# Pairs in the first gate/up block, un-normed operands, and weight sums moved to GpSimd in a transformer block

## The chip, the core and the metric

The kernel runs on one core of one Trainium2 chip. The metric is the device time of one execution in microseconds. The core has five engines that matter here, each with its own queue of instructions that it works off in order: TensorE (PE, matmuls and transposes), VectorE (DVE), ScalarE (ACT), GpSimd (POOL) and the sync engine (SP), which only issues transfers. Engines wait for each other by semaphores.

## The reference

One layer of a hybrid transformer on 256 rows of width 2048, in float32:

```python
h = x + W_out [ DiffAttn(heads) ; ConformerConv(channels) ] ( RMSNorm(x) )
hn = rms_norm(h, norm2_g)                   # h * rsqrt(mean(h*h) + eps) * gain
a  = hn @ w_gate                            # 2048 x 5632
bu = hn @ w_up                              # 2048 x 5632
y  = h + (silu(a) * bu) @ w_down            # 5632 x 2048
```

The change concerns the last four lines, from the point at which h is complete. The norm's factor is one number for each row of h (called rstd2 in the kernel); the gain is one number for each column. So (h * gain) @ w, multiplied by rstd2 row by row afterwards, is the same as hn @ w.

## The kernel before, in words

**Products.** Every float32 product is made of three: each operand is split into a high part in a reduced format (fp32r) and the rest, and x @ w is x_hi w_hi + x_lo w_hi + x_hi w_lo. The rows of h are the stationary operand (two halves of 128 rows, m = 0 and 1), transposed, in 16 slices k of 128 columns. The weights are the moving operand, 512 columns at a time.

**Chunks.** The weights come in chunks of two slices k of 512 columns (128x1024 elements). A chunk is fetched by SP into `raw`, rounded by ScalarE into `whi` (L326), its rest is made by VectorE as `wlo` (L335), and TensorE has 12 products of it (two slices, two halves, three products). For some chunks ScalarE and a GpSimd transfer make `wlo` in VectorE's place (`by_dma`: ScalarE writes the negative of the rounded weights, L329, then a transfer adds `raw`, L330).

**Pairs.** From block 1 on, four of the sixteen slices of gate and up go through a fast scheme: a `pair` takes slice k and slice k+8, gate and up, and needs seven block products (each of three) where plain chunks need eight, so 21 TensorE instructions in place of 24. For it the weights need four sums (`wt`: L1049 with 1024 elements, L1050 and L1051 with 512, of the four raw parts `wb`), the rounding of three raw parts and four sums (`wh`: L1052, L1055) and their rests (`wlb` L1058, `wlt` L1059). The operands of h need seven forms (`make_forms`). The products gather in eight PSUM banks `q`, and after a block's last pair VectorE makes the results from them (`bank_sums`, L1188 to L1193).

**Blocks.** The feed-forward part has eleven gate/up blocks j = 0 to 10 of 512 columns of gate and up each, in groups of 4, 4 and 3; behind each group stand two passes over w_down. A fast block consists of four pairs (s) and eight plain chunks of gate (g) and up (u); their order is a string, `sggsggsuusuu`, and for block 1 `gsggsgsuusuu`. Block 0 is plain before: sixteen chunks with the operands `hhi`, `hlo`, since the forms aren't there yet.

**How block 0 opens.** `out_done(n)` runs when 512 columns of h are complete in PSUM (n = 0 to 3): VectorE adds x (L828), TensorE transposes (L846), ScalarE copies with the gain into `hn` (L851) and casts to `hhi` (L853), VectorE makes `hlo` (L854). For n = 3 also the squares (L479), rstd2, and a copy of h to DRAM (`hd`, by GpSimd). The factor is applied in block 0 after the products (`silu_done`, `up_done`). Meanwhile `make_forms` turns rstd2 into a row through TensorE (`ps_r`), multiplies `hn` by it (L996) and makes `chi`, `clo` and the seven forms for the blocks that follow.

**What sets the order.** The program is written out by a scheduler of generators. It steps through the chunks; for each it first makes the loads, the rounding (`round`) of chunks up to three ahead and the rests (`split`) of chunks up to two ahead, then the products, with a `resume()` in between, which moves every running generator (`out_done`, `make_forms`, `bank_sums` and the like) one `yield` further. `yield from lag(n)` waits n such steps. Each engine then executes its own instructions in exactly that order.

Of the kernel before, what the change touches and what calls it, by code (L numbers as in the profile page):

```python
# [18 lines left out]
P = 128  # L19
# [14 lines left out]
LINE = 128  # L34
EPS = 1e-6
# [51 lines left out]
FIRST_ORDER = "gsggsgsuusuu"  # L87
# [42 lines left out]
def tile_block(  # L130
# [13 lines left out]
    prestack = ExitStack()  # L144
    pre = prestack.enter_context(tc.tile_pool(name="pre", bufs=2))
    small = prestack.enter_context(tc.tile_pool(name="small", bufs=4))
# [4 lines left out]
    h = [pre.tile([P, D], F32, tag=f"h{m}", name=f"h{m}", bufs=1) for m in range(NM)]  # L151
# [325 lines left out]
    def square_sum(src, accum, **kw):  # L477
        junk = pre.tile([P, N], F32, tag="junk", name="junk", bufs=1)
        act.activation(junk[:, : src.shape[-1]], src, AF.Square, accum_out=accum, **kw)  # L479
# [106 lines left out]
    def conv_back(b):  # L586
# [37 lines left out]
        for b in range(2):  # L624
            for t in range(NB // 2):
# [6 lines left out]
                for j in range(2):  # L632
# [3 lines left out]
                    hi = pre.tile([P, S], F32R, tag="mchi", name=f"mchi{ct}", bufs=NCT)  # L636
                    lo = pre.tile([P, S], F32R, tag="mclo", name=f"mclo{ct}", bufs=NCT)
# [135 lines left out]
    def attend_values(hd):  # L773
# [29 lines left out]
        for e in range(2):  # L803
            mixa[2 * hd + e] = lhs_pair("a", 2 * hd + e) if hd >= 2 else tuple(
                pre.tile([P, S], F32R, tag=t, name=t, bufs=4) for t in ("mahi", "malo"))
# [7 lines left out]
    hT = {}  # L813

    hn = []
# [9 lines left out]
    def out_done(n, ps):  # L825
        cs = slice(n * N, (n + 1) * N)
# [13 lines left out]
        for t in range(0, N // P, 2):  # L840
# [6 lines left out]
            if k % HK == 0:  # L847
                hn.append(early.tile([P, HK, S], F32, tag="wb", name="hn"))
            rows = hn[k // HK][:, k % HK : k % HK + 2, :]
            for i in range(2):  # L850
                act.activation(rows[:, i, :], pt[:, i, :], AF.Copy, scale=col("g2", k + i))  # L851
            hi, lo = lhs_two("h", k)
            act.copy(hi, rows)  # L853
            dve.tensor_tensor(lo, rows, hi.bitcast(F32), ALU.subtract)  # L854
            for i in range(2):
                hT[k + i] = (hi[:, i, :], lo[:, i, :])
# [3 lines left out]
        else:  # L860
            yield
            yield
            prestack.close()
            ffn["pool"] = ctx.enter_context(tc.tile_pool(name="ffn", bufs=1))
            start(make_forms())


    ffn = {}
    actT = {}
    sil = {}  # L870

    def silu_done(ps):
        yield
        for m in range(NM):
            sil[m] = ffn["pool"].tile([P, N], F32, tag=f"sum{m}", name="sil")
            act.activation(sil[m], ps[m], AF.Silu, scale=rstd2[m])

    def up_done(j, ps):
# [190 lines left out]
    def multiply_pair(c):  # L1069
        while (fs := c["pairs"]()) is None:  # L1070
            resume()
# [304 lines left out]
```

## The time and the profile before

| | |
|---|---|
| Median of 3 runs | 1032.63 us (1032.61 to 1032.65) |
| Profiled execution, span from first to last instruction | 1030.8 us |
| Profiled execution, time around the span | not shown for itself; the median less the span is 1.8 us |
| TensorE busy | 1025.7 us (100%) |
| VectorE busy | 929.2 us (90%) |
| ScalarE busy | 643.4 us (62%) |
| GpSimd busy | 102.7 us (10%) |
| Granted TensorE clock | 1.000 |

A row of a timeline gives the start in us, the time of the instruction (or of a run of like ones, x4), engine, line, operation, what it writes and reads, the shape, and in brackets how long the engine had been idle and what ended that. TensorE's instructions overlap: a 512-column product is shown with 0.39 us and the next starts 0.23 us later. VectorE's and ScalarE's overlap a little with their follower on the same engine. A row of a window gives the stretch, the sum and the busy time of each engine (with counts), the granted clock, the share of the transfer engines and their rate.

### The profile page before, as it was taken

The numbers are of one execution on the slowest core, as the hardware profiler recorded it, in microseconds if no ns is written. First come the engines' busy times: TensorE is split into PE (matmuls) and PEld (weight loads), VectorE is DVE, ScalarE is ACT, GpSimd is POOL, SyncE is SP. The second block draws the span as 40 slices with busy tenths as digits, with TensorE's granted clock in tenths as the row PEclk, the third lists the DMA queues.
The fourth block names the chain that finished last, engine by engine and source line by source line (L and its number), as shares of the span: only waits on it lengthen the run. The fifth ranks groups of instructions, "written<-read, shape, count | busy, mean of one in ns | idle before, by whom it ended". The sixth has DMA issues, their size and how long they took to land.

```text
span 1030.8 us, 13034 instructions
## 1 busy us (share of the span) xinstructions
PE 1025.7 (100%) x4642; PEld 849.4 (82%) x4642; DVE 929.2 (90%) x1128; ACT 643.4 (62%) x786; POOL 102.7 (10%) x146
## 2 busy tenths in 40 slices
PE   9999999999999999999999999999999999999998
PEld 8888888888888888888888888888888888888887
DVE  6899999999765699999999898989999989889998
ACT  7644656665756675676666556667757556657562
POOL 0300112111000000100102101101001111010020
PEclk9999999999999999999999999999999999999999
DMA  9757555544466677997989799889798979897776
GB/s 338 254 194 258 190 184 164 158 169 166 141 215 214 197 262 222 282 265 210 254 259 272 251 257 270 258 234 262 228 269 255 285 207 283 247 267 218 226 200 174
DMA packets 116448, 238.64 MB, mean 232 GB/s; under 512 B 7840, under 2 KB 9120, under 8 KB 116384
## 3 DMA queue, kind: packets, MB, share of 16 engines
q1 hardware_dynamic: 105216, 203.58, 59.3%
q0 software_dynamic: 10880, 34.08, 17.0%
q8 instruction: 36, 0.59, 0.2%
q14 instruction: 28, 0.23, 0.1%
q10 hardware_dynamic: 288, 0.16, 0.1%
HBM read 204.24 MB, written 9.44 MB: 207 GB/s over the span
## 4 chain that ended last, share of the span: by engine, by line
PE 100%; POOL 0%; DVE 0%; issue 0%; POOLq 0%
PE acc L365 11%; PE acc L366 11%; PE acc L371 11%; PE q L1097 11%; PE q L1103 11%; PE q L1098 11%; PE q L1078 9%; PE q L1077 9%; PE q L1076 9%; PE ps_a L898 1%; PE ps_s L712 1%; PE ps_o L782 1%; PE ps_warm L164 0%; PE ps_h L846 0%; PE ps_qk L693 0%; PE ps_at L802 0%
## 5 line engine op out<-in xcount | busy, mean ns | idle before, releaser
L326 ACT CAST whi<-raw 128x1024 fp32r<-128x1024 f32 (+1 forms) x256 | 264.2, 1043 | 143.8 <-PE acc L366 86.6
L335 DVE TENSOR_TENSOR wlo<-raw,whi 128x1024 fp32r<-128x1024 f32 (+1 forms) x208 | 250.4, 1214 | 38.2 <-ACT whi L326 38.0
L1055 ACT CAST wh<-wt 128x2048 fp32r<-128x2048 f32 x61 | 116.8, 1915 | 109.9 <-DVE wt L1051 109.7
L1059 DVE TENSOR_TENSOR wlt<-wt,wh 128x2048 fp32r<-128x2048 f32 x61 | 139.8, 2291 | 19.8 <-ACT wh L1055 19.7
L1097 PE MATMUL q<-whi,chi 128*128 128x512 f32 x320 | 125.2, 391 | 0.0
L1098 PE MATMUL q<-whi,clo 128*128 128x512 f32 x320 | 124.6, 389 | 0.0
L365 PE MATMUL acc<-whi,xhi 128*128 128x512 f32 x312 | 124.1, 398 | 0.0
L366 PE MATMUL acc<-whi,xlo 128*128 128x512 f32 x312 | 122.2, 392 | 0.0
L1076 PE MATMUL q<-wh,fhi 128*128 128x512 f32 x280 | 109.8, 392 | 0.0
L1077 PE MATMUL q<-wh,flo 128*128 128x512 f32 x280 | 109.0, 389 | 0.0
L1058 DVE TENSOR_TENSOR wlb<-wb,wh 128x1536 fp32r<-128x1536 f32 x61 | 106.8, 1751 | 1.0 <-ACT wh L1052 1.0
L572 DVE SCALAR_TENSOR_TENSOR y<-upad,cw,y 128x256 f32<-128x256 f32 x240 | 101.6, 490 | 0.0
L330 POOL DMA_DIRECT2D wlo<-raw x48 | 41.5, 865 | 555.7 <-ACT wlo L329 286.3
L1052 ACT CAST wh<-wb 128x1536 fp32r<-128x1536 f32 x61 | 89.8, 1472 | 1.0 <-DMA wb<-in_w_down_dram 1.0
L1103 PE MATMUL q<-wlo,chi 128*128 128x512 f32 x320 | 85.7, 390 | 0.0
L371 PE MATMUL acc<-wlo,xhi 128*128 128x512 f32 x312 | 85.2, 394 | 0.0
L1049 DVE TENSOR_TENSOR wt<-wb 128x1024 f32<-128x1024 f32 x61 | 74.4, 1220 | 0.0
L1097 PE MATMUL q<-whi,ahi 128*128 128x512 f32 x182 | 71.0, 390 | 0.0
L1098 PE MATMUL q<-whi,alo 128*128 128x512 f32 x182 | 70.9, 389 | 0.0
L1103 PEld LDWEIGHTS q<-wlo,chi 128*128 128x128 f32 x320 | 60.0, 188 | 12.7 <-DMA wlo<-raw 0.3
L1097 PEld LDWEIGHTS q<-whi,chi 128*128 128x128 f32 x320 | 60.1, 188 | 12.3
L1098 PEld LDWEIGHTS q<-whi,clo 128*128 128x128 f32 x320 | 60.1, 188 | 12.2
(260 smaller groups left out, 1850.5 us busy)
## 6 DMA issues: line engine op xcount, KB each, us to landing
raw<-in_w_in_dram SPq DMA_DIRECT2D x78, 512.0 KB, 4.6
raw<-in_w_gate_dram SPq DMA_DIRECT2D x48, 512.0 KB, 5.0
raw<-in_w_up_dram SPq DMA_DIRECT2D x48, 512.0 KB, 5.3
wlo<-raw POOLq DMA_DIRECT2D x48, 512.0 KB, 7.1
raw<-in_w_down_dram SPq DMA_DIRECT2D x46, 512.0 KB, 6.2
wb<-in_w_down_dram SPq DMA_DIRECT2D x42, 512.0 KB, 5.9
wb<-in_w_up_dram SPq DMA_DIRECT2D x40, 512.0 KB, 4.4
wb<-in_w_gate_dram SPq DMA_DIRECT2D x40, 512.0 KB, 5.5
```

Of the source, the lines that this page charges most:

```text
L326: act.copy(c["hi"], c["raw"])
L335: dve.tensor_tensor(c["lo"], c["raw"], c["hi"].bitcast(F32), ALU.subtract)
L365: pe.matmul(ps[m], xhi[:, ms], hi[:, j, :], start=c["first"] and j == 0, stop=False)
L366: pe.matmul(ps[m], xlo[:, ms], hi[:, j, :], start=False, stop=False)
L371: pe.matmul(ps[m], xhi[:, ms], lo[:, j, :], start=False, stop=c["last"] and j == nk - 1)
L1055: act.copy(c["hi"][:, :SUMMED], c["t"])
L1059: dve.tensor_tensor(lot, c["t"], c["hi"][:, :SUMMED].bitcast(F32), ALU.subtract)
L1076: pe.matmul(ps, hi, c["hi"][:, w], start=bool(first), stop=False)
L1077: pe.matmul(ps, lo, c["hi"][:, w], start=False, stop=False)
L1097: pe.matmul(ps, xs[i][0][:, ms], hi[:, i, :], start=i == 0 and bool(c["first"].get(qs[m])), stop=False)
L1098: pe.matmul(ps, xs[i][1][:, ms], hi[:, i, :], start=False, stop=False)
L1103: pe.matmul(sum_bank(c, qs[m]), xs[i][0][:, ms], lo[:, i, :], start=False, stop=i == 1 and bool(c["last"].get(qs[m])))
```

## The change

What it does, in the order of the program:

1. **Operands without the factor.** The transposed h with the gain, but not rstd2, is written by ScalarE straight to `chi`, the rest by VectorE to `clo` (for the slices of the plain chunks), and to `rows` for the slices of the pairs. `make_forms` starts when three quarters of h are complete, since the pairs' slices lie in the first three quarters, and has no factor, no `ps_r` and no multiplication any more. rstd2 is applied in `products_done` of every block: Silu with the factor as its scale, then a copy of the result with the same scale (the products of gate and up each carry the factor once).
2. **Pairs in block 0.** Block 0 is a fast block with the order `gugsgsgsusuu`; its PSUM banks come from the two pools the other way round (`swap`), and no wlo is made by a transfer in it. `round_pair` steps the generators until the forms and the memory (`late`) are there.
3. **A pair's VectorE work** is cut into smaller pieces and interleaved: 1024 elements of `wt` in `round_pair`, then `wlb` 512, `wt` 512, `wlb` 1024, `wt` 512, and `wlt` in two halves of 1024. ScalarE casts the sums in two halves too.
4. **Bank sums** in an order in which no sum needs the one just ahead of it, but for the first ones.
5. **GpSimd** makes the three `wt` sums of the next pair that hasn't been rounded (`sums_aside`), written out behind the bank sums; that holds for 14 of the 65 pairs.
6. The memory pools are laid out anew: what was freed at once before block 0 is freed in two steps, at the first and the last 512 columns of h.

```diff
-FIRST_ORDER = "gsggsgsuusuu"
+ORDERS = {0: "gugsgsgsusuu", 1: "gsggsgsuusuu"}
...
     def out_done(n, ps):
+        if not n:
+            prestack.close()
+            ffn["pool"] = fp = ctx.enter_context(tc.tile_pool(name="ffn", bufs=1))
...
-            if k % HK == 0:
-                hn.append(early.tile([P, HK, S], F32, tag="wb", name="hn"))
-            rows = hn[k // HK][:, k % HK : k % HK + 2, :]
-            for i in range(2):
-                act.activation(rows[:, i, :], pt[:, i, :], AF.Copy, scale=col("g2", k + i))
-            hi, lo = lhs_two("h", k)
-            act.copy(hi, rows)
-            dve.tensor_tensor(lo, rows, hi.bitcast(F32), ALU.subtract)
+            if k % HK < NS:
+                rows = ffn["rows"][:, k // HK, k % HK : k % HK + 2, :]
+                for i in range(2):
+                    act.activation(rows[:, i, :], pt[:, i, :], AF.Copy, scale=col("g2", k + i))
+            else:
+                a = REST.index(k)
+                hi, lo = (ffn[x][:, a : a + 2, :] for x in ("chi", "clo"))
+                for i in range(2):
+                    act.activation(hi[:, i, :], pt[:, i, :], AF.Copy, scale=col("g2", k + i))
+                for i in range(2):
+                    dve.scalar_tensor_tensor(lo[:, i, :], pt[:, i, :], col("g2", k + i), hi[:, i, :].bitcast(F32),
+                                             ALU.mult, ALU.subtract)
+                    plain[k + i] = (hi[:, i, :], lo[:, i, :])
             yield
...
+        if n == HK * P // N:
+            yield
             start(make_forms())
+        if n == D // N - 1:
+            yield
+            yield
+            keepstack.close()
+            ffn["late"] = ctx.enter_context(tc.tile_pool(name="late", bufs=1, side="right"))
...
     def round_pair(c):
-        assert "pair" in forms
+        while "pair" not in forms or "late" not in ffn:
+            resume()
...
+    def first_sums(c, engine):
+        b = c["b"]
+        c["t"] = t = ffn["pool"].tile([P, 4, N], F32, tag="wt", name="wt")
+        engine.tensor_tensor(t[:, 2:4], b[:, 1:3], b[:, 0:1].to_broadcast([P, 2, N]), ALU.subtract)
+
+    def last_sums(c, engine):
+        b, t = c["b"], c["t"]
+        yield engine.tensor_tensor(t[:, 1], b[:, 1], t[:, 3], ALU.add)
+        yield engine.tensor_tensor(t[:, 0], t[:, 1], b[:, 3], ALU.subtract)
+
+    def sums_aside():
+        pairs = [c for c in chunks if c.get("kind") == "s"]
+        n = next((n for n, c in enumerate(pairs) if not c.get("rounded")), None)
+        if n and "b" in pairs[n] and "lo" in pairs[n - 1]:
+            c = pairs[n]
+            first_sums(c, pool)
+            c["summed"] = len(list(last_sums(c, pool)))
...
     def split_pair(c):
-        act.copy(c["hi"][:, :SUMMED], c["t"])
...
-        dve.tensor_tensor(lob, c["b"][:, 1:], c["hi"][:, SUMMED:].bitcast(F32), ALU.subtract)
-        dve.tensor_tensor(lot, c["t"], c["hi"][:, :SUMMED].bitcast(F32), ALU.subtract)
+        act.copy(hi[:, 2:SUMMED], t[:, 2:])
+        rest(lob[:, :1], b[:, 1:2], hi[:, SUMMED : SUMMED + 1])
+        next(sums, None)
+        rest(lob[:, 1:], b[:, 2:], hi[:, SUMMED + 1 :])
+        next(sums, None)
+        act.copy(hi[:, :2], t[:, :2])
+        rest(lot[:, 2:], t[:, 2:], hi[:, 2:SUMMED])
+        rest(lot[:, :2], t[:, :2], hi[:, :2])
...
     def bank_sums(q):
         act.copy(w1, q[Q1])
         yield
         dve.tensor_tensor(u2, q[Q6], w1, ALU.add)
+        dve.tensor_tensor(w1, q[Q2], w1, ALU.add)
         dve.tensor_tensor(u3, q[Q7], u2, ALU.add)
+        dve.tensor_tensor(u2, q[Q5], u2, ALU.add)
         dve.tensor_tensor(w4, q[Q5], u3, ALU.add)
-        dve.tensor_tensor(u2, q[Q5], u2, ALU.add)
-        dve.tensor_tensor(w1, q[Q2], w1, ALU.add)
         dve.tensor_tensor(u3, q[Q4], u3, ALU.add)
+        sums_aside()
...
-        for t in g:
-            act.activation(t, t, AF.Silu)
+        for m, t in enumerate(g):
+            act.activation(t, t, AF.Silu, scale=rstd2[m])
+            act.activation(t, t, AF.Copy, scale=rstd2[m])
...
-            if j:
-                gate_up_block(j)
-                continue
-            block(w_gate, j * N, range(KD), fh, silu_done)
-            block(w_up, j * N, range(KD), fh, lambda ps, j=j: up_done(j, ps))
+            gate_up_block(j)
```

How it moves instructions, at three places: where block 0 begins, where it ends, and GpSimd's queue. Names end in the number of the buffer.

TensorE where block 0 begins, before: the last transposes of h (`ps_h`) stand in two groups of four; this is the first group, between the first and the second chunk of block 0 (`hhi`, `hlo`).

```order
L365 MATMUL acc<-whi,hhi_2958 128x512
L366 MATMUL acc<-whi,hlo_2959 128x512
L371 MATMUL acc<-wlo,hhi_2958 128x512 x4
L846 MATMUL ps_h<-ident,h_81 128x128
L846 MATMUL ps_h<-ident,h_82 128x128
L846 MATMUL ps_h<-ident,h_81 128x128
L846 MATMUL ps_h<-ident,h_82 128x128
L365 MATMUL acc<-whi,hhi_2983 128x512
```

The same place in the change, from the last products of w_out (`mchi`) on:

```order
L374 MATMUL acc<-wlo,mchi_2869 128x512
L374 MATMUL acc<-wlo,mchi_2875 128x512
L852 MATMUL ps_h<-ident,h_88 128x128
L852 MATMUL ps_h<-ident,h_89 128x128
L852 MATMUL ps_h<-ident,h_88 128x128
L852 MATMUL ps_h<-ident,h_89 128x128
L852 MATMUL ps_h<-ident,h_88 128x128
L852 MATMUL ps_h<-ident,h_89 128x128
L852 MATMUL ps_h<-ident,h_88 128x128
L852 MATMUL ps_h<-ident,h_89 128x128
L1094 MATMUL q_3371<-whi,chi 128x512
```

All eight transposes now stand between the last product of w_out and the first product of block 0, which reads the operands `chi`.

VectorE in the same stretch of the change, from the sums of h (L834) through the rest of the first pair:

```order
L834 TENSOR_TENSOR h_88<-h_88,acc 128x512
L834 TENSOR_TENSOR h_89<-h_89,acc 128x512
L842 TENSOR_REDUCE ssh<-ss_0_143 128x1
L842 TENSOR_REDUCE ssh<-ss_1_144 128x1
L863 SCALAR_TENSOR_TENSOR clo<-ps_h,cols,chi 128x256 x4
L1025 TENSOR_TENSOR wt<-wb 128x1024
L338 TENSOR_TENSOR wlo<-raw,whi 128x1024
L1047 TENSOR_TENSOR wlb<-wb,wh 128x512
L1029 TENSOR_TENSOR wt<-wb,wt 128x512
L1047 TENSOR_TENSOR wlb<-wb,wh 128x1024
L1030 TENSOR_TENSOR wt<-wt,wb 128x512
L1047 TENSOR_TENSOR wlt<-wt,wh 128x1024 x2
```

Before, `hlo` of two slices and the wlo of plain chunks stood here, and the first pair's work some thirty instructions later; now the pair's work follows the correction `clo` directly.

VectorE in the change where block 0 ends: the bank sums of block 0, and the rest of block 1's first pair behind them. Its first sum (L1025) stands ahead of these rows.

```order
L1187 TENSOR_TENSOR sum_3662<-q_3466,sum_3661 128x512
L1188 TENSOR_TENSOR sum_3661<-q_3470,sum_3661 128x512
L1189 TENSOR_TENSOR sum_3663<-q_3470,sum_3662 128x512
L1190 TENSOR_TENSOR sum_3662<-q_3374,sum_3662 128x512
L1047 TENSOR_TENSOR wlb<-wb,wh 128x512
L1029 TENSOR_TENSOR wt<-wb,wt 128x512
L1047 TENSOR_TENSOR wlb<-wb,wh 128x1024
L1030 TENSOR_TENSOR wt<-wt,wb 128x512
L1047 TENSOR_TENSOR wlt<-wt,wh 128x1024 x2
L1208 TENSOR_TENSOR sum_3661<-q_3399,sum_3661 128x512
```

Before, block 0 had no bank sums, only the two products with the factor (L883) behind that pair's `wlt`; now the pair's rest stands behind six bank sums, of which the last four are shown.

GpSimd in the change, from the first blocks on: the sums stand between the transfers that make `wlo`, and one of them waits behind each set of three.

```order
L333 DMA wlo<-raw 128x1024 x3
L1025 TENSOR_TENSOR wt<-wb 128x1024
L1029 TENSOR_TENSOR wt<-wb,wt 128x512
L1030 TENSOR_TENSOR wt<-wt,wb 128x512
L333 DMA wlo<-raw 128x1024 x4
```

Before, fifteen such transfers stood in a row here, with nothing between them.

More of the change, by code (lines that the diff above doesn't have):

```diff
@@ new lines, in split_pair, with rest @@
+    def split_pair(c):
+        hi, b, t = c["hi"], c["b"], c["t"]
+        lob = ffn["late"].tile([P, 7 - SUMMED, N], F32R, tag="wlb", name="wlb", bufs=2)
+        lot = ffn["late"].tile([P, SUMMED, N], F32R, tag="wlt", name="wlt", bufs=2)
+        sums = iter(()) if c.get("summed") else last_sums(c, dve)
+        def rest(lo, raw, h):
+            dve.tensor_tensor(lo, raw, h.bitcast(F32), ALU.subtract)
+        act.copy(hi[:, 2:SUMMED], t[:, 2:])
[6 more added lines that the diff above has]
+        rest(lot[:, :2], t[:, :2], hi[:, :2])
@@ L1131, in multiply_two, with fast_block @@
             start(c["done"](c["sums"]))
-    def fast_block(order, pairs, twos, sources, operands, half, whole, by_dma=dict(g=(), u=())):
+    def fast_block(order, pairs, twos, sources, operands, half, whole, by_dma=dict(g=(), u=()), swap=False):
         units, sums = [], {}
@@ L1138, in fast_block @@
             what = left[kind].pop(0)
-            c = dict(kind=kind, sums=sums, done=None, first={}, last={}, rows=what["rows"], **operands)
+            c = dict(kind=kind, sums=sums, swap=swap, done=None, first={}, last={}, rows=what["rows"], **operands)
             if kind == "s":
@@ L1158, in gate_up_block @@
     def gate_up_block(j):
[L1159 removed]
+        fast_block(ORDERS.get(j, ORDER), [dict(p=p, rows=slice(p, p + HK + 1, HK)) for p in range(NS)],
                    [dict(ks=ks, rows=slice(ks[0], ks[1] + 1, ks[1] - ks[0]), k=ks) for ks in TWOS],
                    dict(g=(w_gate, j * N), u=(w_up, j * N)),
[L1162 removed]
+                   dict(pairs=lambda: forms.get("pair"), plain=plain.get),
                    products_done, lambda sums: block_done(j, sums),
[L1164 removed]
+                   BY_DMA if j > 1 and j not in FIRSTS else dict(g=(), u=BY_DMA["u"] if j else ()), swap=not j)
     def down_pass(g, j0, nb):
@@ L1183, in bank_sums @@
     def bank_sums(q):
-        w1, u2, u3, w4 = (ffn["pool"].tile([P, N], F32, tag=f"sum{i}", name=f"sum{i}") for i in range(4))
+        w1, u2, u3, w4 = (ffn["late"].tile([P, N], F32, tag=f"sum{i}", name=f"sum{i}") for i in range(4))
         act.copy(w1, q[Q1])
```

102 lines of the change are left out of this document (27 added, 75 removed).

## The prediction

> **What bounds the kernel now.** I read the page's header and chain first, then the waits, then the stretches of time, then the timeline where the change begins.
>
> ```profile
> span 1030.8 us, 13034 instructions
> PE 1025.7 (100%) x4642; PEld 849.4 (82%) x4642; DVE 929.2 (90%) x1128; ACT 643.4 (62%) x786; POOL 102.7 (10%) x146
> PEclk9999999999999999999999999999999999999999
> PE 100%; POOL 0%; DVE 0%; issue 0%; POOLq 0%
> 340.00:385.00 45.00, 45.00 (x205) 37.13 (x204) 38.04 (x40) 31.20 (x41) 1.99 (x4) 1.00 0.70 229
> 385.00:480.00 95.00, 95.00 (x431) 78.63 (x430) 89.59 (x86) 63.93 (x61) 6.97 (x8) 1.00 0.86 253
> ```
>
> The chain that ended last is TensorE from end to end, at full granted clock, and in the last two rows (columns: the stretch, its sum, PE, PEld, DVE, ACT, POOL) PE is busy for the whole of each stretch: 340 to 385 is block 0, 385 to 480 the blocks behind it. So only fewer TensorE instructions can make this kernel faster, and whatever makes TensorE wait is paid in full. VectorE has little to spare: 38.04 of 45 us in block 0, 89.59 of 95 us behind it. The profiled execution has a span of 1030.8 us; the median of the runs, 1032.63 us, holds some 1.8 us around it, which the change leaves alone. I add differences to the median.
>
> **What leaves TensorE.** Block 0 had 16 plain chunks of 12 products; now it has 8 plain chunks and 4 pairs of 21, which is 180 products of 512 columns for 192. The two transposes of the norm's factor (ps_r) go too.
>
> ```profile
> 337.40 1.07 PE L371 MATMUL acc<-wlo,mchi 128*128 128x512 f32 x4
> 338.31 0.39 PE L365 MATMUL acc<-whi,hhi 128*128 128x512 f32 x1
> 340.12 1.07 PE L371 MATMUL acc<-wlo,hhi 128*128 128x512 f32 x4
> 341.03 0.67 PE L846 MATMUL ps_h<-ident,h 128*128 128x128 f32 x4
> 341.46 0.48 PE L365 MATMUL acc<-whi,hhi 128*128 128x512 f32 x1
> 343.40 0.60 PE L846 MATMUL ps_h<-ident,h 128*128 128x128 f32 x4
> 344.76 0.39 PE L365 MATMUL acc<-whi,hhi 128*128 128x512 f32 x1
> ```
>
> The chunk from 338.31 to 341.03 takes 2.72 us, so a product costs 0.227 us (the 0.39 of a row overlaps the next) and a pair of 21 costs 4.76 us. Twelve products are 2.72 us. The chunk that holds the eight transposes runs from 341.03 to 344.76, 3.73 us for 2.72, so a transpose costs 0.126 us and two cost some 0.25 us. Together **-2.95 us**. Since TensorE never waited here before, that is also the most that can be gained, unless the rows hide a wait that I don't see.
>
> **The opening of block 0.** Before, the last eight transposes of h stood behind 12 products of block 0 (341.03, against 338.31 where block 0 begins), and that first chunk hid the way from the last w_out product through VectorE's sum. Now they stand directly behind the last w_out product.
>
> ```profile
> 338.69 1.23 DVE L335 TENSOR_TENSOR wlo<-raw,whi 128x1024 fp32r<-128x1024 f32 x1 [1.49 <-ACT whi L326]
> 339.83 1.28 DVE L828 TENSOR_TENSOR h<-h,acc 128x512 f32<-128x512 f32 x2
> 340.54 0.63 ACT L479 ACTIVATE junk<-h 128x512 f32<-128x512 f32 x1 [1.89 <-DVE h L828]
> 341.30 0.63 ACT L479 ACTIVATE junk<-h 128x512 f32<-128x512 f32 x1
> 341.93 0.82 ACT L851 ACTIVATE hn<-ps_h,cols 128x256 f32<-128x256 f32 x2
> 342.78 0.62 ACT L853 CAST hhi<-hn 128x512 fp32r<-128x512 f32 x1
> ```
>
> The four products from 337.40 finish two of one bank, then two of the other. The first bank is done at 337.40+0.23+0.39 = 338.02, so the first sum runs 338.06 to 338.74 (half of 1.28 with its overlap: 0.68, the next 0.60 behind it) and the second ends at 339.34. The first four transposes can go at 338.78, the second of them needs 339.38, and eight of them end some 0.88 us later: 340.26, for 339.32 without a wait. **Stall A: 0.94 us.** Whether the first sum waits for the first bank or for all four products (338.47) decides between 0.9 and 1.4.
>
> **The first pair.** Its weights' sums and casts now stand on VectorE and ScalarE behind that same chain. ScalarE: two squares, 0.76 apart (340.54 to 341.30), from 338.78 to 340.30; four copies of ps_h, 0.82 for two, to 341.95. VectorE: four 256-column corrections to some 342.4, then the pair's row of work and one plain chunk's wlo. These are the rows of one pair before, and its TensorE rows:
>
> ```profile
> 618.96 1.22 DVE L1049 TENSOR_TENSOR wt<-wb 128x1024 f32<-128x1024 f32 x1
> 620.21 0.69 DVE L1050 TENSOR_TENSOR wt<-wb,wt 128x512 f32<-128x512 f32 x1
> 621.55 1.75 DVE L1058 TENSOR_TENSOR wlb<-wb,wh 128x1536 fp32r<-128x1536 f32 x1
> 623.61 2.29 DVE L1059 TENSOR_TENSOR wlt<-wt,wh 128x2048 fp32r<-128x2048 f32 x1 [0.31 <-ACT wh L1055]
> 625.98 0.69 DVE L1188 TENSOR_TENSOR sum<-q,sum 128x512 f32<-128x512 f32 x1
> 629.35 0.68 DVE L1193 TENSOR_TENSOR sum<-q,sum 128x512 f32<-128x512 f32 x1
> 631.44 1.29 DVE L1209 TENSOR_TENSOR sum<-q,sum 128x512 f32<-128x512 f32 x2 [1.41 <-PE q L1103]
> 626.25 0.39 PE L1097 MATMUL q<-whi,chi 128*128 128x512 f32 x1
> 630.22 1.14 ACT L1201 ACTIVATE sum<-sum 128x512 f32<-128x512 f32 x2
> ```
>
> The split halves are not in this trace; I price 1024 elements at 1.13 us from start to start (338.69 to 339.83) and 1.22 alone, 512 at 0.60 and 0.69. First sum 342.4 to 343.6; wlo to 344.7; wlb's 512, wt's 512, wlb's 1024, wt's 512 to 347.7; ScalarE's cast of that (1024 elements, 1.05) to 348.75; the second half of wlt from 348.8 to 349.96. TensorE, 0.94 late, has done its three plain chunks (3 x 2.72) at 348.42 and needs that half in the pair's third product, at 348.87. **Stall B: 1.1 us.** A and B share one chain: if A is smaller, B grows by as much, so 2.05 is the sum of both, and both bounds belong to the sum. Low: every step of the chain overlapped so that only A is left, 0.9. High: the halves of wlb take the place of h in the on-chip memory, so they wait until h has been written out.
>
> ```profile
> hd<-h POOLq DMA_DIRECT2D x2, 256.0 KB, 3.9
> wlo<-raw POOLq DMA_DIRECT2D x48, 512.0 KB, 7.1
> ```
>
> Issued at some 339.6 and 3.9 us long it lands at 343.5, a microsecond before the first wlb; at the 7.1 of GpSimd's other transfers it would land at 346.7 and cost 2.0 more: 4.1.
>
> **Pairs 2 to 4 of block 0.** Each comes with one plain chunk: TensorE 4.76+2.72 = 7.48 us. VectorE has five 1024s and three 512s, 5x1.13+3x0.60 = 7.45, plus 0.03 to 0.05 for each of the two results that the next one waits for: 7.54. **Stall C: 3x0.06 = 0.2 us**, from 0 (the slack of the plain chunk behind) to 1.0 (0.3 of semaphore latency in each round).
>
> **Into block 1.** The order puts block 0's six bank sums ahead of the rest of block 1's first pair. In the rows, the sums begin 0.27 ahead of the end of the last pair (625.98 against 626.25) and take 4.05. The pair's rest behind them is 0.60+0.60+1.13+0.69, the cast 1.05, the last half 1.22 and 0.1 between: 5.4, so it is ready 9.15 us behind the pair's end. TensorE needs it after three plain chunks and two products, 8.16+0.45 = 8.61. **Stall D: 0.5** (0 to 1.5). Then the block's own transposes stand 12 products into the next pair; ScalarE now has four dependent steps ahead of them (Silu, and the gate times the factor, for both halves), at 0.57 each from the Silu row, behind a 1.05 cast. That and VectorE's product end some 0.5 us late. **Stall E: 0.5** (0 to 1.2).
>
> Sum: -2.95 + 0.94 + 1.1 + 0.2 + 0.5 + 0.5 = **+0.3 us**. Bounds: -2.95+0.9 = -2.05, and -2.95+4.1+1.0+1.5+1.2 = +4.85.
>
> **What costs nothing.** In every later block VectorE's cost for a pair is the same, cut smaller (each cut adds some 0.1 us: 1.13+0.60 for 1.75, 2x1.13 for 2.29), and 14 pairs lose 1.22+0.69+0.69 = 2.6 us from VectorE to GpSimd. TensorE waited for neither, so this buys nothing. The added gate copies are ScalarE's (62% busy). GpSimd's prices have only small rows:
>
> ```profile
> 36.40 0.46 POOL L200 TENSOR_TENSOR gcsq<-rt,gb 128x128 f32<-128x128 f32 x1
> 36.82 0.32 POOL L201 TENSOR_TENSOR gcsq<-rt,gb 128x64 f32<-128x64 f32 x1
> 37.10 1.30 POOL L202 TENSOR_TENSOR gcsq<-rt,gb 128x64 f32<-128x64 f32 x1
> 36.90 1.32 DVE L335 TENSOR_TENSOR wlo<-raw,whi 128x1024 fp32r<-128x1024 f32 x1 [1.71 <-ACT whi L326]
> 630.80 0.86 POOL L330 DMA_DIRECT2D wlo<-raw  x1 [4.10 <-ACT wlo L329]
> 641.46 1.07 PE L1103 MATMUL q<-wlo,chi 128*128 128x512 f32 x4
> ```
>
> 64 elements more cost 0.14 us, so 1024 cost some 2.4, 512 some 1.3, all three some 5 us: 626.0 to 631.0. The bank sums take 4.05 of it on VectorE. The third row shows the risk: the same 64 elements take 1.30 us instead of 0.32 when VectorE's two-operand pass over on-chip weights starts at 36.90. The bank sums read a bank and one such operand, and GpSimd runs beside them. Behind the three sums in GpSimd's queue stands the next wlo transfer, before at 630.80, landing 7.1 later at 637.9 and needed at 641.46: 3.5 us to spare. The Trainium skill, "SBUF — State Buffer", section "Who interferes with whom", goes further than the row: a VectorE instruction with two SBUF inputs and a GpSimd instruction that reads SBUF exclude each other, and whichever comes second waits for the whole of the first, so VectorE can be the one that waits. By that rule a late 1024-element sum would hold VectorE for up to its 2.4 us; the 2.6 us that each such pair takes off VectorE cover it, and the sum stays the same. In the rows VectorE lost 0.1 (1.32 for 1.22).
>
> **The rivals.** *Slower through GpSimd.* If the sums end more than 3.5 us behind 631, the wlo transfer is late, and TensorE waits at each of 14 places. It takes sums 1.7 times as long as I have them, and the row 1.30 for 0.32 shows that collisions cost that and more. For it speaks that row; against it that VectorE's passes at that time read banks. At 0.5 us a place: +0.3+7 = 1039.9 us. *Slower in block 0.* The upper ends of A to E together, with h's write-out as the wait that decides, from a landing later than 344.5 on: at two thirds of the way +3.4, 1036.0 us. *Faster.* ScalarE and VectorE overlap more than I replay, only A and a little is left: -2.95+0.9 and 0.1 for the rest, 1030.7 us at the most; for it speaks that VectorE idles 1.49 us ahead of 338.69, against it that A alone is 0.9 by the rows. *The sums on GpSimd do nothing*: that is in the forecast already.
>
> **Chances.** A measurement of this kernel tells about 0.2%, 2.07 us, from no change. Forecast (within that) 0.50; faster by more 0.18; slower through block 0 0.20; slower through GpSimd 0.12. So faster 0.18, same 0.50, slower 0.32. The likeliest time is 1032.63+0.3 = 1032.9 us; its own range is 1030.6 (lower bound) to 1034.7. To leave out no more than 2 in 10, the range goes from 1030.4 to 1036.5.
>
> **What would show it.** In the profile after: the waits must show PE idle before ps_h on VectorE's sum of h (A, 0.4 to 0.9), before a wlt of block 0 (B, some 1.1) and before ps_a of block 0 (E); PE's count must fall by 14. GpSimd's three sums should take some 5 us and PE should wait for no wlo. The forecast falls if PE waits in the blocks behind, if A and B together come under 1 us, or if wlb waits for h's transfer.

## The result, and the profile after

The changed kernel takes 1049.09 us (median of 4 runs, 1045.96 to 1050.36) against 1032.62 us: ratio 1.0156, 95% interval 1.0139 to 1.0173. I had forecast 1032.9 us, no measurable change, with 1030.4 to 1036.5 as the range. It is slower by 16.5 us, well outside. The profile below is of the slowest of the four executions (1050.36 us), so the losses read from it add up to 17.8 us, not 16.5.

The page of the changed kernel: the span, the engines, and the chain that ended last.

```profile
span 1048.6 us, 13217 instructions
PE 1030.9 (98%) x4628; PEld 848.7 (81%) x4628; DVE 922.7 (88%) x1230; ACT 666.7 (64%) x861; POOL 174.1 (17%) x188
PE 17%; DVE 3%; issue 2%; DMA 2%; POOL 1%; ACT 0%; DVEq 0%; POOLq 0%; ACTq 0%
```

TensorE has the 14 instructions less that the forecast counted (4628 for 4642), yet it is busy for 5 us longer, and the chain is no longer TensorE alone. What it waited for (us in total, times, longest us):

```profile
PE q L1100 <- DMA wlo<-raw: 4.5, 3, 4.1
PE q L1094 <- DVE sum L1190: 1.9, 1, 1.9
PE ps_h L852 <- DVE h L834: 1.7, 2, 1.5
...
PE q L1073 <- ACT wh L1054: 1.3, 1, 1.3
```

Before, the only wait was 1.4 us at the start of the kernel. Behind the start of the kernel, all the waits come to 11.0 us, where 16.5 us and the saved 2.95 had to be lost. Much of the rest lies in the clock. The stretches behind three of the waits (stretch, sum, then busy time of PE, PEld, DVE, ACT, POOL, then the granted clock):

```profile
352.00:356.00 4.00, 3.36 (x8) 2.71 (x9) 4.00 (x6) 2.55 (x3) 0.00 (x0) 0.58 0.94 307
356.00:360.00 4.00, 4.00 (x19) 3.29 (x19) 4.00 (x5) 2.32 (x3) 0.00 (x0) 1.00 0.45 115
972.00:978.00 6.00, 5.38 (x17) 4.26 (x18) 6.00 (x8) 4.71 (x5) 0.00 (x0) 0.72 0.40 139
1018.00:1026.00 8.00, 5.76 (x15) 4.55 (x16) 8.00 (x10) 4.27 (x5) 0.05 (x1) 0.57 1.01 219
```

At half clock a product takes 0.43 us instead of 0.23, which counts as busy. So TensorE can be busier with less to do. In the profile before, the clock is 1.00 throughout.

Set against each other, the two timelines give the place of the loss. The offset is the start of the same piece of work after, less before:

| place | before | after | offset |
|---|---|---|---|
| last products of w_out | 337.40 | 337.61 | +0.2 |
| first product of block 1 | 383.10 | 386.50 | +3.4 |
| first pass of the third group begins | 963.94 | 970.06 | +6.1 |
| its third chunk | 969.74 | 979.73 | +10.0 |
| last pass, third chunk, wlo products | 1005.46 | 1020.24 | +14.8 |
| the pair behind it | 1006.36 | 1022.11 | +15.8 |
| end of the span | 1030.8 | 1048.6 | +17.8 |

Without the saved 2.95 us, block 0 alone lost 6.2 us (3.4-0.2+2.95). The blocks between lost 2.7: 1.2 at block 1, and some 0.5 at each of three places (439.61, 761.64 and 814.06) where a wlo transfer came late. The third group's first pass lost 3.9, the last pass and the end 7.8. Block 0 and the two passes hold most of it, and these are their rows.

**Block 0's opening**, VectorE, then TensorE:

```profile
334.33 1.75 DVE L1000 TENSOR_TENSOR flo<-sums,fhi 128x1536 fp32r<-128x1536 f32 x1
336.00 3.49 DVE L338 TENSOR_TENSOR wlo<-raw,whi 128x1024 fp32r<-128x1024 f32 x3
339.41 1.28 DVE L834 TENSOR_TENSOR h<-h,acc 128x512 f32<-128x512 f32 x2
...
347.06 0.69 DVE L1047 TENSOR_TENSOR wlb<-wb,wh 128x512 fp32r<-128x512 f32 x1 [0.77 <-DMA hd<-h]
```

```profile
340.15 0.33 PE L852 MATMUL ps_h<-ident,h 128*128 128x128 f32 x1 [1.46 <-DVE h L834]
...
351.23 0.50 PE L1073 MATMUL q<-wh,fhi 128*128 128x512 f32 x1 [1.31 <-ACT wh L1054]
351.56 0.40 PE L1074 MATMUL q<-wh,flo 128*128 128x512 f32 x1
352.64 0.76 PE L1075 MATMUL q<-wlt,fhi 128*128 128x512 f32 x1 [0.68 <-issue]
```

h's last sum starts at 339.41, not at 338.06: the forms' work (the flo row is its end) now lies ahead of it and VectorE is behind with three passes over plain weights. The first pair then waits for its sums, and its products run at half clock until 355.8.

**The third group's first pass.** GpSimd's sums (first two rows) meet VectorE's passes over its forms and weights:

```profile
961.10 2.73 POOL L1025 TENSOR_TENSOR wt<-wb 128x1024 f32<-128x1024 f32 x1
963.91 1.50 POOL L1029 TENSOR_TENSOR wt<-wb,wt 128x512 f32<-128x512 f32 x1
```

```profile
961.05 4.78 DVE L966 TENSOR_TENSOR dls<-dsums,dhs 128x384 fp32r<-128x384 f32 x2
965.75 2.30 DVE L338 TENSOR_TENSOR wlo<-raw,whi 128x1024 fp32r<-128x1024 f32 x1
```

The same two groups of VectorE before:

```profile
954.38 1.02 DVE L971 TENSOR_TENSOR dls<-dsums,dhs 128x384 fp32r<-128x384 f32 x2
955.32 1.22 DVE L335 TENSOR_TENSOR wlo<-raw,whi 128x1024 fp32r<-128x1024 f32 x1
```

VectorE lost 4.8 us here, its bank sums came late, and TensorE waited 1.9 us for a bank (L1190 in the waits).

**The last pass.** ScalarE, then the transfer that it holds up, then TensorE:

```profile
1007.29 1.05 ACT L1054 CAST wh<-wt 128x1024 fp32r<-128x1024 f32 x1 [6.18 <-DVE wt L1030]
...
1009.20 1.05 ACT L332 ACTIVATE wlo<-raw 128x1024 fp32r<-128x1024 f32 x1
```

```profile
1010.62 0.88 POOL L333 DMA_DIRECT2D wlo<-raw  x1 [11.92 <-ACT wlo L332]
```

```profile
1020.24 2.08 PE L1100 MATMUL q<-wlo,ahi 128*128 128x512 f32 x4 [4.14 <-DMA wlo<-raw]
```

ScalarE stands 6.18 us before a cast whose input, the last of a pair's sums, VectorE now makes behind the bank sums. The negated wlo stands behind that cast in ScalarE's queue, and the transfer behind it: issued at 1010.62, it is wanted by 1016.1 and lands at 1020.20. Before, the cast came without a wait and the transfer was issued at 995.15, for products that began at 1005.46:

```profile
990.11 1.92 ACT L1055 CAST wh<-wt 128x2048 fp32r<-128x2048 f32 x1
995.15 0.88 POOL L330 DMA_DIRECT2D wlo<-raw  x1 [6.49 <-ACT wlo L329]
1005.46 1.07 PE L1103 MATMUL q<-wlo,ahi 128*128 128x512 f32 x4
```

Set against the offset of 10.0 us at this point, the issue is 5.5 us late. The transfer itself also took longer, 9.6 us for 6.0 before. So late issue and slow transfer both feed the wait. The four transfers that add to h in memory now stand right behind it (from 1011.18 and 1012.27; before, from 995.70 and 999.09); whether they slowed it, no run here separates.

### The profile page after: what moved, and what is told of

Read it like the earlier page. It is cut to its first block, busy times and chain, and to the rows that moved or that the text cites. A ratio compares the mean times of both kernels' runs of the same rounds, so it can differ in the third digit from the quotient of the medians.

```text
span 1048.6 us, 13217 instructions
## 1 busy us (share of the span) xinstructions
PE 1030.9 (98%) x4628; PEld 848.7 (81%) x4628; DVE 922.7 (88%) x1230; ACT 666.7 (64%) x861; POOL 174.1 (17%) x188
## 5 line engine op out<-in xcount | busy, mean ns | idle before, releaser
L329 ACT CAST whi<-raw 128x1024 fp32r<-128x1024 f32 (+1 forms) x248 | 255.7, 1043 | 124.8 <-PE acc L369 69.6
L338 DVE TENSOR_TENSOR wlo<-raw,whi 128x1024 fp32r<-128x1024 f32 (+1 forms) x200 | 242.8, 1224 | 39.8 <-ACT whi L329 39.6
L1047 DVE TENSOR_TENSOR wlt<-wt,wh 128x1024 fp32r<-128x1024 f32 x130 | 156.8, 1222 | 9.6 <-ACT wh L1049 9.6
L1047 DVE TENSOR_TENSOR wlb<-wb,wh 128x512 fp32r<-128x512 f32 (+1 forms) x130 | 124.1, 963 | 22.0 <-ACT wh L1018 21.1
L1054 ACT CAST wh<-wt 128x1024 fp32r<-128x1024 f32 x65 | 68.5, 1053 | 114.0 <-DVE wt L1030 109.3
L1094 PE MATMUL q<-whi,chi 128*128 128x512 f32 x352 | 137.8, 391 | 0.0
L1095 PE MATMUL q<-whi,clo 128*128 128x512 f32 x352 | 137.0, 389 | 0.0
L1073 PE MATMUL q<-wh,fhi 128*128 128x512 f32 x308 | 121.4, 394 | 1.3 <-ACT wh L1054 1.3
L1074 PE MATMUL q<-wh,flo 128*128 128x512 f32 x308 | 120.4, 391 | 0.0
L1100 PE MATMUL q<-wlo,chi 128*128 128x512 f32 x352 | 94.3, 390 | 0.3 <-DMA wlo<-raw 0.2
L1049 ACT CAST wh<-wt 128x1024 fp32r<-128x1024 f32 x65 | 68.3, 1051 | 22.3 <-DVE wt L1025 22.1
L1094 PEld LDWEIGHTS q<-whi,chi 128*128 128x128 f32 x352 | 66.1, 188 | 13.6
```

The costliest lines, as they stand in the source:

```text
L329: act.copy(c["hi"], c["raw"])
L338: dve.tensor_tensor(c["lo"], c["raw"], c["hi"].bitcast(F32), ALU.subtract)
L1047: dve.tensor_tensor(lo, raw, h.bitcast(F32), ALU.subtract)
L1073: pe.matmul(ps, hi, c["hi"][:, w], start=bool(first), stop=False)
L1074: pe.matmul(ps, lo, c["hi"][:, w], start=False, stop=False)
L1094: pe.matmul(ps, xs[i][0][:, ms], hi[:, i, :], start=i == 0 and bool(c["first"].get(qs[m])), stop=False)
```

## The experiments

Times are medians, ratios against the kernel before run on the same chip, with 95% intervals.

### Taking parts out of the change

No sums on GpSimd:

```diff
         dve.tensor_tensor(u3, q[Q4], u3, ALU.add)
-        sums_aside()
```

> The change without GpSimd's weight sums: VectorE makes the sums of all 65 pairs, everything else as in the change. Theory: three separate losses make up the 16.5 us. (1) The opening of block 0 and its passage into block 1, some 7 us against my forecast of the gain; (2) GpSimd's sums, which hold VectorE in the third group's first down pass (its dls took 4.8 us for 1.0) and put wlo transfers behind them in three places, some 5 us; (3) the last two sums of a pair, which now stand late in VectorE's order, so that ScalarE waits for them in the last down pass and a wlo transfer starts late, some 6.5 us. By it this run is some 5 us faster than the change: 1044 us (1042 to 1046), and the wait for wlo in the last down pass stays. Rival, GpSimd is the whole cause behind block 0: then that wait goes as well and it comes to 1037 to 1039 us.

1045.2 us (1.0120, 1.0104 to 1.0135): 3.9 us faster than the change, near the 5 expected. TensorE's wait for a bank is gone, the wait for wlo in the last pass stays (3.7 us). So GpSimd isn't the cause of that one. Nor is it the cause of one of the three late transfers between: its wait stands here at 759.79 (0.20 us), in the change at 761.64 (0.16). A slow clock stretch moved: here it lies behind the wait ahead of ps_h (1.47 and 0.27 us, the same as in the change), and the first pair runs at full clock.

```profile
341.00:345.00 4.00, 4.00 (x15) 3.19 (x14) 2.99 (x7) 3.23 (x8) 1.23 (x3) 0.58 0.90 309
```

All three sums at the rounding, GpSimd kept:

```diff
         if "t" not in c:
             first_sums(c, dve)
+            c["summed"] = len(list(last_sums(c, dve)))
```

> The change with one edit: the second and third sum of a pair's weights stand directly behind the first, where the pair is rounded, as before, and no longer between the rests. GpSimd still makes the sums of its 14 pairs. Theory of three losses: ScalarE no longer waits for the late sum in the last down pass, its wlo starts some 5 us earlier, loss (3) goes: 1042.5 us (1041 to 1044.5); the collision of GpSimd with VectorE in the third group's first down pass stays (1048's dls rows of over 2 us). Rival, the late transfer is due to GpSimd's queue: no difference, 1047 to 1050 us.

1038.6 us (1.0064, 1.0049 to 1.0079): 10.5 us faster, where 6.5 were expected. The wait for wlo in the last pass is gone; a shorter one, 2.0 us for a pair's weights, stands there now. What I hadn't expected is that VectorE no longer lost to GpSimd either, although GpSimd still made its sums. The rows of the same place, GpSimd and VectorE:

```profile
956.47 5.48 POOL L1026 TENSOR_TENSOR wt<-wb 128x1024 f32<-128x1024 f32 x1
```

```profile
957.07 1.02 DVE L966 TENSOR_TENSOR dls<-dsums,dhs 128x384 fp32r<-128x384 f32 x2
958.01 1.22 DVE L338 TENSOR_TENSOR wlo<-raw,whi 128x1024 fp32r<-128x1024 f32 x1
```

This time VectorE was in the middle of a run of passes when GpSimd's sum came, and GpSimd's sum took 5.48 us instead of 2.73 while VectorE ran at its usual speed. Which of the two pays changes with the moment.

Both edits together:

> Both edits: no sums on GpSimd, and all three sums of a pair where the pair is rounded. Theory of three losses: only the opening and the passage into block 1 are left, 1037.5 us (1036 to 1039), and behind block 1 TensorE waits nowhere. Rival, the smaller pieces or the scaled gate on ScalarE cost something by themselves behind block 1: then waits of TensorE stay there and it comes to 1040 us or more.

1040.43 us (1.0077, 1.0060 to 1.0094), 3 us above what I expected and where the rival had it, and not to be told from the one before (its runs went from 1038.39 to 1041.02, these from 1038.59 to 1040.77). Its waits:

```profile
PE q L1076 <- DVE wlt L1048: 3.0, 2, 2.2
PE ps_h L852 <- DVE h L834: 1.7, 2, 1.5
PE q L1076 <- issue: 1.6, 1, 1.6
```

The opening is there as expected (1.7 and 1.6 us), and TensorE falls another 1.1 us behind at block 1 (0.8 of it a wait). The wait of 2.2 us lies in the last pass, like the 2.0 us of the run before: the weights of a pair, issued at 999.41, landed after 13.6 us; in the kernel before the same transfer took 9.3. The smaller pieces aren't its cause, since the run with whole pieces (block 0's part alone, below) has it too, with 1.6 us; the scaled gate on ScalarE is in both runs, so this part of the rival stays open.

### Single parts put into the kernel before

GpSimd's sums alone (the same `sums_aside` behind the bank sums, the other pairs' sums early as before):

> The kernel before with GpSimd's sums alone: three sums of the next unrounded pair behind the bank sums, on 14 pairs; block 0, operands and a pair's VectorE work as before. Theory: GpSimd costs only where its turn collides with VectorE's own passes or puts a wlo transfer too late; with the sums of the other pairs made early, as in this kernel, that is seldom: 1033.5 us (1032.5 to 1035), TensorE waits for a wlo at most in two or three places of some 0.4 us. Rival, GpSimd is itself what costs the change its time behind block 0: 1037 us or more, with waits at most block ends.

1033.95 us (1.0014, 1.0005 to 1.0024), 10 runs. A cost of 1.5 us; behind the start of the kernel TensorE waits at one place, the third group's first pass again:

```profile
965.46 0.47 PE L1110 MATMUL q<-whi,ahi 128*128 128x512 f32 x1 [1.16 <-DVE sum L1205]
```

GpSimd there, then VectorE:

```profile
953.58 2.72 POOL L1056 TENSOR_TENSOR wt<-wb 128x1024 f32<-128x1024 f32 x1
```

```profile
953.65 3.07 DVE L964 SCALAR_TENSOR_TENSOR dlo<-raw_act,dhi 128x384 fp32r<-128x384 f32 x1
956.65 1.64 DVE L966 TENSOR_TENSOR dlo<-dsums,dhi 128x384 fp32r<-128x384 f32 x1
```

GpSimd's sum begins 0.07 us ahead of VectorE's dlo, and dlo takes 3.07 us instead of 0.55.

The same with the sums of that one pair left to VectorE:

> The kernel before with GpSimd's sums for the first 13 of the 14 pairs: the one left out is the pair of the third group's first down pass, where GpSimd's sums ran against VectorE's own two-operand passes (dlo 3.07 us for 0.55, dls 2.11 for 1.02). Theory: that one collision is what GpSimd's sums cost by themselves, 1.2 us of TensorE's wait: 1032.7 us, within 0.4 of the kernel before, and 1.2 us below the 1033.95 with all 14. Rival, the cost is spread over the other 13 places: 1033.5 us or more.

1033.06 us (1.0006, 0.9997 to 1.0015), 11 runs: 0.9 us less, expected were 1.2 (the two runs are from different chips). In its profile TensorE waits nowhere behind the start of the kernel. The median lies between the theory's 1032.7 and the rival's 1033.5, and 0.6 us above the kernel before on the same chip, with an interval that holds no change. So the thirteen other pairs cost nothing that can be told from the noise, and show no gain.

The late sums and the cut pieces alone:

```diff
     def round_pair(c):
-        dve.tensor_tensor(t[:, 1], b[:, 1], t[:, 3], ALU.add)
-        dve.tensor_tensor(t[:, 0], t[:, 1], b[:, 3], ALU.subtract)
     def split_pair(c):
-        act.copy(c["hi"][:, :SUMMED], c["t"])
-        dve.tensor_tensor(lob, c["b"][:, 1:], c["hi"][:, SUMMED:].bitcast(F32), ALU.subtract)
-        dve.tensor_tensor(lot, c["t"], c["hi"][:, :SUMMED].bitcast(F32), ALU.subtract)
+        act.copy(hi[:, 2:SUMMED], t[:, 2:])
+        rest(lob[:, :1], b[:, 1:2], hi[:, SUMMED : SUMMED + 1])
+        dve.tensor_tensor(t[:, 1], b[:, 1], t[:, 3], ALU.add)
+        rest(lob[:, 1:], b[:, 2:], hi[:, SUMMED + 1 :])
+        dve.tensor_tensor(t[:, 0], t[:, 1], b[:, 3], ALU.subtract)
+        act.copy(hi[:, :2], t[:, :2])
+        rest(lot[:, 2:], t[:, 2:], hi[:, 2:SUMMED])
+        rest(lot[:, :2], t[:, :2], hi[:, :2])
```

> The kernel before with the new cut of a pair's VectorE work alone: two of a pair's three sums stand between its rests, ScalarE casts them in two halves; GpSimd makes no sums, block 0 is plain. Theory: the late sums delay ScalarE in the last down pass, and with it one wlo transfer, by some 5 us, with TensorE at half its clock behind the wait: 1038 us (1036 to 1040). Rival, the late transfer needs the shift of block 0 or GpSimd as well: 1033 us, no wait of TensorE.

1039.68 us (1.0070, 1.0055 to 1.0085): 7.3 us by this part alone, with neither block 0 nor GpSimd. The wlo transfer is issued at 1000.84 instead of 995.15 and takes 9.1 us instead of 6.0. TensorE's timeline agrees with the kernel before within 0.7 us up to the last pass; there stand the same rows as in the change.

```profile
997.51 1.06 ACT L1065 CAST wh<-wt 128x1024 fp32r<-128x1024 f32 x1 [6.14 <-DVE wt L1064]
```

```profile
PE q L1111 <- DMA wlo<-raw: 3.9, 2, 3.7
```

Block 0's part alone (the change with a pair's work whole and early as before, no sums on GpSimd; left are the operands without the factor, block 0's pairs and the order of the bank sums):

> The change with all of a pair's work as before (three sums at the rounding, rests of 1536 and 2048 elements, one cast), and no sums on GpSimd: only block 0's pairs, the operands without the factor and the order of the bank sums are left of the change. Theory: the opening of block 0 (4.5 us of waits for 2.95 of gain) and 0.5 to 1 us at block 1 stay, and the wait of 2.2 us for a pair's weights in the last down pass, whose transfer took 13.6 us among the others there, may come or go with the moment: 1036 us (1034.5 to 1039). Rival, the cut pieces cost by themselves: 1034 us and no wait in the last pass.

1040.31 us (1.0075, 1.0058 to 1.0092), above the 1036 expected and its range. That is 7.9 us for block 0's part. The three parts put singly into the kernel before, or left alone of the change, cost 1.5+7.3+7.9 = 16.7 us; the change costs 16.5. That the sum comes out is partly chance, for the parts don't simply add: this run waits 1.10 us for a wlo transfer at 512.90 and 1.59 us for a pair's weights in the last pass, which the change's profile doesn't show, and taking parts out of the change saved 3.9 us (GpSimd), 10.5 (late sums) and 8.7 (both). The run also shows what the cut is good for: whole, the pairs of block 0 follow each other on VectorE every 8.0 us (wlt at 349.01, 357.01 and 365.01), with 0.3 us of idle time for ScalarE's cast; cut, every 7.55 us.

### Block 0

Another order of block 0, five plain chunks first:

```diff
-ORDERS = {0: "gugsgsgsusuu", 1: "gsggsgsuusuu"}
+ORDERS = {0: "gugugsgssusu", 1: "gsggsgsuusuu"}
```

> As the one before, and block 0 in another order: five plain chunks ahead of its first pair, g u g u g s g s s u s u, for g u g s g s g s u s u u. The pair's rounding then no longer pulls the last transposes of h ahead of block 0's first products: they stand behind 12 and 20 of them, as before the change. Theory: the stall at the opening comes from the transposes' place and from the first pair's chain, both go; with 2.95 us less of TensorE work and about 1 us of waits left it comes to 1031 us (1029.8 to 1033). Rival, VectorE is short of time in block 0 wherever its pairs stand, since two of them now follow each other: then TensorE waits in the pairs, and it comes to 1035 us or more.

1040.87 us (1.0076, 1.0061 to 1.0091), no better than 1040.43. The transposes of h stand behind 12 products again, and TensorE waits 0.3 us for them instead of 1.7. But the first pair is still late by 1.2 us, the third, which follows the second without a plain chunk, by 2.0, and block 1 begins with 1.4 us of waiting for a bank. The rival held: VectorE is short of time (busy for 42.59 us from 340 to 385, where it was 38.04 before), and the order only says where. A part of the first pair's wait is again h's way to memory (0.61 us of VectorE).

The same with VectorE relieved (three wlo by transfer, forms one step earlier, whole pieces; of the edit only the line for the wlo is shown):

```diff
-                   BY_DMA if j > 1 and j not in FIRSTS else dict(g=(), u=BY_DMA["u"] if j else ()), swap=not j)
+                   BY_DMA if j > 1 and j not in FIRSTS else dict(g=(), u=BY_DMA["u"]) if j else dict(g=TWOS[3:], u=TWOS[2:]), swap=not j)
```

> As the one before, and the opening eased on VectorE: block 0 in the order g u g u g s g s s u s u (transposes of h behind 12 products), the forms made one step earlier and in fewer steps, and the wlo of three late plain chunks of block 0 by transfer in place of VectorE. Theory: block 0 is short of VectorE time; with 3 x 1.13 us less in it and h's last sum some 2 us earlier, block 0 and block 1 wait 1.5 to 3 us for 2.95 of gain: 1032 us (1031 to 1034.5). Rival, the chain from h's last sum to the first pair (squares, copies, sums, h's way out to memory) sets the opening whatever VectorE's load: 1035 us or more, with the wait at the first pair as long as in the order tried before (1.2 us) and two more behind it.

1040.33 us (1.0078, 1.0063 to 1.0093); a miss by 8 us. The first pair was late by 1.0 us, the third by 1.9, and one of the transferred wlo landed 1.3 us late: it was issued at 376.47 and took 8.4 us. This one doesn't separate the chain from VectorE's load, since three things were changed together.

The rests of the forms left out (GpSimd writes zeros, so the forms' low parts are missing from the result):

> The change without GpSimd's sums and with a pair's three sums at its rounding, and without VectorE's rests of the seven forms (six passes, some 5.3 us of VectorE ahead of h's last sum; GpSimd writes zeros in their place, so the forms' low parts are missing from the result). Theory: at the opening TensorE waits for VectorE's backlog, which the forms' work, moved ahead of h's last sum, makes: h's sum then starts some 1.3 us earlier (338.1 instead of 339.4 on the profile's clock) and the first pair's wait shrinks too; the two stalls of 1.9 and 1.9 us come to 2.1 together, the sum I forecast, and block 1 begins some 1.7 us earlier. Total 1038.5 us or less against the 1040.4 of the same kernel with the rests. Rival, the opening hangs on the chain behind h's last sum and on h's way out to memory alone: h's sum and block 1 move by less than 0.5 us.

1038.29 us (1.0054, 1.0039 to 1.0069). VectorE's rows at the opening, for the same kernel with the rests and then without:

```profile
335.77 3.49 DVE L338 TENSOR_TENSOR wlo<-raw,whi 128x1024 fp32r<-128x1024 f32 x3
339.18 1.28 DVE L834 TENSOR_TENSOR h<-h,acc 128x512 f32<-128x512 f32 x2
```

```profile
335.76 1.23 DVE L338 TENSOR_TENSOR wlo<-raw,whi 128x1024 fp32r<-128x1024 f32 x1 [0.68 <-ACT whi L329]
337.85 1.28 DVE L834 TENSOR_TENSOR h<-h,acc 128x512 f32<-128x512 f32 x2 [0.86 <-PE acc L374]
```

h's sum comes 1.33 us earlier and now waits for TensorE, as I had forecast it for the change; block 1 begins 1.3 us earlier (383.35 for 384.66). TensorE's wait ahead of ps_h falls from 1.7 to 0.6 us. The first pair's wait did not shrink (1.6 us in both), so the 1.7 expected were 1.3. The median is within the 1038.5 expected.

### The last pass, and the forms

In the last group, the transfers that add the first pass's sums to h in memory (hd<-sum) four steps later; GpSimd's sums are out and a pair's sums made at the rounding, as in the run with both edits:

```diff
-            yield from lag(HD_LAG)
+            yield from lag(HD_LAG if g < 2 else HD_LAG + 4)
```

> The change without GpSimd's sums and with a pair's three sums at its rounding; beside it, in the last group, the transfers that add the first pass's gate sums to h in memory are issued four steps later, behind those of the up sums. Theory: the wait of 2.2 us for a pair's weights in the last down pass comes from the transfers crowded there (that pair's second half took 13.6 us to land, 9.3 before the change): with two of the accumulating transfers later it lands in 10 us or less, the wait goes, and the kernel comes to 1038 us. Rival, the crowding is of the loads themselves, whatever the order: the half still takes 12 us or more, 1040 us.

1036.28 us (1.0034, 1.0021 to 1.0047): 4.1 us faster than with both edits, more than expected (2.6 us between the two profiled executions). The pair's second half landed after 9.3 us instead of 13.6, and TensorE doesn't wait in the last pass any more. So in this variant the order of these transfers decides. Why the half took 13.6 us in that run and 9.3 in the kernel before, with the same transfers issued in the same order and at distances that agree within 0.5 us, no run here tells.

With the forms begun a step earlier on top:

> The one before, with the forms begun one step earlier and made in one step less, and h's last sum and squares written out at once with the last product of w_out. Theory: the idle time of VectorE ahead of its first form (2.4 us, twice) is used in part, so h's last sum starts up to 1 us earlier, and block 1 begins 0.5 to 1 us earlier than in that one: 1037 us. The kernel before (1032.4 us) is not reached, since VectorE is still short of some 4 us in block 0. Rival, no effect, because the passes over plain weights that stand ahead of h's sum can't start earlier: within 0.3 us at block 1.

1037.29 us (1.0042, 1.0025 to 1.0059), no gain on the run before. The number is near the 1037 expected, but not by the theory. h's last sum didn't come earlier (339.81): the passes over plain weights ahead of it are four instead of three. And the first pair took 9.1 us for 4.76, with 2.5 us of waiting in one piece, so that block 1 began at 387.21, 2.5 us later than in the run before, where it was to begin 0.5 to 1 us earlier.

No version beat the kernel before. The best with block 0's pairs is the 1036.28.

## Why the prediction was wrong

**What leaves TensorE: right.** 14 instructions less. With the waits out of it, that would be 2.95 us.

**Stall A, 0.94 us: the step that failed at the opening.** It measured 1.46 and 0.27 us. I took h's last sum to start as soon as the bank was there (338.06); it started at 339.41. I knew that the forms begin when three quarters of h are complete, but the sum has no term for this VectorE work, which stands ahead of h's last sum and fills VectorE up to it. The run without the forms' rests gives the sum at 337.85 and a wait of 0.6, so the chain was right, and what was missing is VectorE's backlog of 1.3 us.

**Stall B, 1.1 us, and that A and B share one sum of 2.05: wrong.** B measured 1.31+0.68 = 1.99 us of waiting, and another 1.95 us in which the pair's products ran at half clock (7.39 us for the pair, less 0.68 and 4.76). The wait on h's way to memory was real, 0.77 us of VectorE, where I had it landing a microsecond early: it was issued at 340.39, not 339.6, and took 6.0 us, not 3.9, inside the upper bound that I had given it. Nor do A and B trade against each other: without the forms' rests A's wait fell by 1.1 us and the first pair's stayed at 1.6.

**C to E: about right.** C was nothing, the other three pairs run in 4.76 us; D 0.20 for 0.5, E 0.46 for 0.5 (of waiting; TensorE fell 1.2 us behind at block 1, for 1.0).

**"What costs nothing": the largest error.** I weighed the cut pieces by their elements and found no TensorE wait that VectorE's time could cause. I did not look at what the moved sums are moved past: the six bank sums on VectorE, and on ScalarE the cast, behind which the next wlo is negated. In the last pass that made a transfer start 5 us late. That part alone costs 7.3 us, shown by putting it alone into the kernel before; in the profile of that run 3.7 us of it are TensorE's wait and some 1.7 the half clock behind it.

**GpSimd: a rival, right in kind and wrong in place.** I priced its queue (the transfer behind the sums) and gave the collision with VectorE 2.4 us, covered by 2.6 that VectorE saves. The sums took 2.74 and 1.30 us (forecast 2.4 and 1.3). Three places had a wlo transfer late, some 0.5 us each, and one of the three is there without GpSimd's sums too. One place had the collision, and it cost VectorE 4.8 us, because the sum ran not beside the bank sums but ahead of them. In the kernel before, that place costs TensorE 1.2 us of waiting, in the change some 4 with the half clock. That is nowhere near 14 places.

**The clock: not in the sum at all.** Every wait in the forecast was priced at its length. In the change three waits were followed by 3 to 5 us of products at half clock. An estimate of the clock's deficit, from the stretches shown above, is 4x0.42+6x0.28+8x0.43 = 6.8 us (part of it while TensorE was waiting anyway). This probably is also why the change's runs spread over 4.4 us, where those of the kernel before beside them agree within 0.2: the two runs of 1050.3 us had a granted clock of 0.993 and 0.995, the two faster ones 0.997.

## What to carry to other kernels

Where one engine is busy all the time, count for a moved instruction not its duration but what it is moved past on its own engine, and then what stands in the queue of the engine that waits for it: two sums of 0.69 us cost 7.3 us here, because a cast, a negation and a transfer stood in line behind them and the clock fell behind the wait. When work is made earlier on an engine, look for the next thing on that engine that TensorE waits for. And where TensorE never waits, relieving another engine wins nothing: the sums of 13 pairs, taken off VectorE in the kernel before, brought no gain.

## What the runs showed of the hardware

**The clock.** TensorE fell to half clock behind waits of 2 us and less: in the change behind 1.31 and 0.68 us within 3 us and behind 1.85 us, in the run without GpSimd's sums behind 1.47 and 0.27 us. But the same wait doesn't always do it. The opening's 1.46 to 1.48 and 0.27 us stand in six profiles. In three the granted clock fell behind them (0.71 from 340 to 344 without GpSimd's sums, 0.57 with whole pieces, 0.57 with the later transfers); in the change and in the runs with the sums early, with and without GpSimd's, it stayed at 1.00. Waits in one piece of 1.6 us and of 2.2 us, in the run with both edits, had no such effect either. What decides, no run here shows. The products at half clock last 3 to 5 us. The Trainium skill, "TensorE: Matmul & The Clock Gate", Part 1, has the clock watched over free-running windows of some 3.4 us, with an idle window behind which it halves; that one and the same wait tells on the clock only at times fits a free-running window, but the waits named here were shorter than a window.

**GpSimd and VectorE.** A GpSimd sum of 1024 elements that begins 0.07 us ahead of a VectorE pass with two operands from on-chip memory holds that pass for the sum's whole time (3.07 us for 0.55); one that comes into a run of such passes waits until the run ends (5.48 for 2.73). The Trainium skill, "SBUF — State Buffer", section "Who interferes with whom", has the two exclude each other for a whole instruction, with the order of issue deciding who waits; both cases are in these rows. That a whole run of VectorE's passes holds GpSimd until its end is what the second row adds. Beside the bank sums, which read a bank and one such operand, both run at their usual speed (GpSimd's 512 elements in 1.29 us, VectorE's bank sums in 0.69, in the run with the sums early).
